# HGRN's heads taken two at a time, and a shorter triangle solve for the sample, in a hybrid RWKV-7 / HGRN2 layer

## The chip, the cores and the metric

The kernel runs on one core of one Trainium2 chip. The metric is the device time of one execution in microseconds, median of several runs. A core has a matmul engine (TensorE, PE in the profile; PEld is its loading of weights), VectorE (DVE), ScalarE (ACT), GpSimd (POOL), and SyncE (SP), from whose queue the data transfers are issued.

## The reference

One decoder layer in float32, for a prompt of 2,048 tokens (one sequence) and for a sample of 8 sequences of 8 new tokens that bring states with them. The input goes through a projection of width 1,024 to 3,840, then through two mixers side by side: RWKV-7 with 8 heads of 64, and HGRN2 with 4 heads of 128. Their outputs are joined, projected, added to the input and normalised, and an MLP of width 4,096 with a squared ReLU follows. HGRN2 is, in chunks:

```python
dec = jnp.exp(jnp.where(mask[:, :, None], diff, -jnp.inf))
att = jnp.einsum('bhtk,bhsk,bhtsk->bhts', qc, kc, dec)
o = jnp.einsum('bhts,bhsv->bhtv', att, ic) + jnp.einsum('bhtk,bhkv->bhtv', qc * jnp.exp(bc), S)
S = jnp.exp(blast[:, :, 0, :])[..., None] * S + jnp.einsum('bhsk,bhsv->bhkv', kc * jnp.exp(blast - bc), ic)
```

RWKV-7 updates a matrix state token by token, S = S diag(w) + (S a) b' + v k', and reads y = S r. In chunks of tokens this needs the inverse of a unit triangular matrix for each chunk and head.

## The kernel before, in words

**Stages.** The prompt is cut into 4 blocks of 512 tokens (`NBLK`, `BT`); block 0 carries the sample's 64 tokens too. `gemm` computes the input projection, block by block, in the order of `SEQ` (low rank rows, RWKV's r, k, v by pairs of heads, HGRN's input i, then f and q of heads 0 and 1, g of these, and so on), and then the output projection (`out_proj`) of the four blocks. Each product is three matmuls of high and low halves (`xh`, `xl`, `wh`, `wl`). Beside it run the streams `rwkv` with its helpers and `hgrn`. After all of that the MLP runs (`mlp_phase`).

**Order.** The order of instructions on each engine is fixed when the kernel is built. Every stream is a generator that issues some instructions and yields; `Sched.run` keeps a clock for each engine from prices in ns (`em.ops`) and lets the ready stream of the best priority go on. The RWKV chain comes first, then HGRN, and the projection is the filling. `Ring` hands out tiles: `RAW` has 12 tiles of 512 columns for x, r, k, f, q, g; `MB` has 3 PSUM banks; `HT` has the two HGRN work tiles (`ht` in the profile). Prices: `em.mm(..., price=35)` for a small HGRN matmul, `RETILE` 115 for a new tile shape.

**HGRN.** `hgrn` (L1577) goes through the heads of a block in turn, and after block 0 through the sample (`hg_sample`). `hg_head` (L1339) makes the forget gate `fg` and, in place of f, the key K, then Q. The attention inside 128 tokens is built in levels: a first batch of matmuls (`within`, L1332: for 4 chunks of 128 tokens, 4 products of 32 columns) gives the diagonal, and level `lv` gives the pairs of blocks of 2^lv tokens. After each level half of Q's columns and half of K's are multiplied by products of the gate (on VectorE, K also on GpSimd, `em.either`), and `fsm` gets the products of neighbours on GpSimd. Levels 0 to 4 use `within` and a masked copy (`copy_predicated`, L1366) into `attd`; levels 5 and 6 use matmuls of 32 and of 64 columns whose results ScalarE copies. So a head has eight batches of small matmuls: the first, five of levels 0 to 4, and one each of levels 5 and 6. Behind the levels come the transpose of K, the state's update, the output, its norm and its gate.

**The reserve.** When head `SPARE_AT` = 3 of block 0 is reached, `smp["rest"]` becomes 4: from then on whoever takes a RAW tile (the evacuations, `evac_job` L695, and the loads of x, `x_loads` L432) leaves four, until `hg_sample` has taken four.

**RWKV.** Nine quads follow each other through one `Stage`: two per block, and the sample as the third. For each, rows are made (`rwkv_rows`), scores computed (`rwkv_scores`), the triangles solved (`rwkv_solve`, L983), and then the chain over chunks runs (`chain`, for the sample `sample_chain`). The solve works on 32x32 triangles with 31 steps of two VectorE instructions (the products into `tmp`, tile `rhsb` in the profile, and their sum into the triangle, tile `xt`), transposes, and a join of the two halves of a 64-token chunk by 32x32 matmuls. The sample's 64 tokens of a head take the same way, though only blocks of 8 tokens belong together.

Of the kernel before, what the change touches and what calls it, by code (L numbers as in the profile page):

```python
# [42 lines left out]
TAIL = {"PE": 213, "DVE": 135, "ACT": 160, "POOL": 75, "SP": 0}  # L43
BUBBLE = 127
RETILE = 115
STEPS = 8
# [287 lines left out]
def mixer_phase(tc, em, a, o, dram, z, banks, sch, begin):  # L334
    nc = tc.nc
# [5 lines left out]
    def tl(shape, name, dt=F32):  # L341
        return rpool.tile(shape, dt, name=name)
# [38 lines left out]
    ET = Ring(sch, [tl([128, 512], f"et{i}") for i in range(ET_N)])  # L381
    HT = Ring(sch, [tl([128, 512], f"ht{i}") for i in range(2)])
    att = tl([128, 512], "att")
    attd = tl([128, 4, 32], "attd")
    em.memset(att, 0.0)
# [27 lines left out]
    for h in range(4):  # L413
        em.memset(Sh[h], 0.0)
    fsms = [tl([128, 512], f"fsm{i}") for i in range(1)]
    rsts = [tl([128, 8], f"rst{i}") for i in range(1)]
    GST = Ring(sch, [tl([128, 16], f"gst{i}") for i in range(2)])
# [565 lines left out]
    def rwkv_solve(sg, nb):  # L983
# [8 lines left out]
        tmp = rhs2[0][64:128]  # L992
        for s in range(31):
            nt, ncol = 31 - s, s + 1
            tv = tmp[:, 0:nt * ncol].rearrange("p (t c) -> p t c", t=nt)
            em.tt(tv, A3[:, s + 1:32, s:s + 1].to_broadcast([64, nt, ncol]),
                  X3[:, s, 0:ncol][:, None, :].to_broadcast([64, nt, ncol]), OP.mult)
            em.tt(X3[:, s + 1:32, 0:ncol], X3[:, s + 1:32, 0:ncol], tv, OP.add)
            if s % SOLVE_STEP == SOLVE_STEP - 1:
                yield "on"  # L1000
        uf = sg.uv.rearrange("p c l x -> p (c l x)")
        x11, w = uf[0:32, 0:1024], uf[32:64, 0:1024]
        tr32(x11.rearrange("t (b c) -> t c b", c=32), X3[0:32].rearrange("b t c -> b c t"))
        for hf in range(2):
            hs = slice(32 * hf, 32 * hf + 32)
            tr32(xt[hs, :, hs].rearrange("c b t -> c t b"), X3[hs])
        yield

# [16 lines left out]
        MB.put(ps)  # L1025
        em.memset(uf[0:64], 0.0)
        em.memset(X3, 0.0)
        em.memset(X3.rearrange("p t c -> p (t c)")[:, 0:1024:33], 1.0)
        yield

# [300 lines left out]

    def within(ps, K, Q):  # L1332

        for c in range(4):
            for x in range(0, 128, 32):
                s = slice(c * 128 + x, c * 128 + x + 32)
                em.mm(ps[x:x + 32, c * 32:c * 32 + 32], K[:, s], Q[:, s], price=35)

    def hg_head(h, b):  # L1339
        yield from sch.wait(("h", b, h))  # L1340
        yield from sch.wait(("i", b))
        fsm, rst = fsms[0], rsts[0]
        q, f = units[b, "q", h], units[b, "f", h]
        its = [units[b, "i", m] for m in range(4)]
        fg, Q = yield from HT.get_all(2)
        em.act(fg, f, AF.Identity, scale=col(P_OML + h), bias=col(P_LBV + h))
        em.act(f, f, AF.Identity, scale=col(P_NOML + h), bias=col(P_OML + h))
        K = f
        em.stt(Q, q, 0.5, fg, OP.mult, OP.mult)
        ps = yield from MB.get()  # L1350
        within(ps, K, q)
        yield
        a3 = att.rearrange("p (c t) -> p c t", c=4)
        em.stt(attd, ps[:, 0:128].rearrange("p (c t) -> p c t", c=4), 0.5,
               cst[:, C_IC:C_IC + 32][:, None, :].to_broadcast([128, 4, 32]), OP.mult, OP.mult)
        MB.put(ps)
        RAW.put(q)
        yield
        cur, off, n = fg, 0, 512
        for lv in range(7):  # L1360
            hh = 1 << lv
            ps = yield from MB.get()
            if lv < 5:
                within(ps, K, Q)
                yield
                nc.vector.copy_predicated(attd, hmask[:, M_LV + 32 * lv:M_LV + 32 * lv + 32][:, None, :].to_broadcast([128, 4, 32]),  # L1366
                                          ps[:, 0:128].rearrange("p (c t) -> p c t", c=4))
                em.ops.append((DVE, 220))
                if lv == 4:
                    for x in range(0, 128, 32):  # L1370
                        em.act(a3[x:x + 32, :, x:x + 32], attd[x:x + 32], AF.Copy)
            else:
                for c in range(4):
                    for x in range(0, 128, 2 * hh):
                        em.mm(ps[x:x + hh, c * hh:c * hh + hh], K[:, c * 128 + x:c * 128 + x + hh], Q[:, c * 128 + x + hh:c * 128 + x + 2 * hh])
                yield
                for x in range(0, 128, 2 * hh):
                    em.act(a3[x:x + hh, :, x + hh:x + 2 * hh], ps[x:x + hh, 0:4 * hh].rearrange("p (c t) -> p c t", c=4), AF.Copy)
            MB.put(ps)
            Q4 = Q.rearrange("p (b x h) -> p b x h", x=2, h=hh)  # L1380
            K4 = K.rearrange("p (b x h) -> p b x h", x=2, h=hh)
            nbk = 512 // (2 * hh)
            fe = cur[:, off:off + n:2][:, :, None].to_broadcast([128, nbk, hh])
            fo = cur[:, off + 1:off + n:2][:, :, None].to_broadcast([128, nbk, hh])
            em.tt(Q4[:, :, 1, :], Q4[:, :, 1, :], fe, OP.mult)
            em.either(K4[:, :, 0, :], K4[:, :, 0, :], fo, OP.mult, E_LATE)
            noff = 0 if lv == 0 else off + n
            em.tt(fsm[:, noff:noff + n // 2], cur[:, off:off + n:2], cur[:, off + 1:off + n:2], OP.mult, eng=POOL)
            cur, off, n = fsm, noff, n // 2
            yield  # L1390
        ft = fsm[:, off:off + 4]
        kt = fg
        ps = yield from MB.get()
# [5 lines left out]
        MB.put(ps)  # L1399
        RAW.put(K)  # L1400
        yield
        hs = slice(h * 128, h * 128 + 128)
        ps = yield from MB.get()
        for c in range(4):
            s = slice(c * 128, c * 128 + 128)
            em.mm(ps[:, s], kt[:, s], its[c][:, hs])
        sr = fsm
        po = yield from MB.get()
# [33 lines left out]
        MB.put(po)  # L1442
        HT.put(Q)
        yield
# [12 lines left out]
        RAW.put(g, delay=ST_TIME)  # L1457
        HT.put(kt)
        yield "go"

    def hg_sample():
# [4 lines left out]
        fsm, rst = fsms[0], rsts[0]  # L1466
        fg, Q = yield from HT.get_all(2)
        qm, s0, s1, im = yield from RAW.get_all(4)
# [92 lines left out]
        RAW.put(s0, s1, im)  # L1561
        HT.put(kt, Qs)
        RAW.put(qm, smp["qf"], smp["g"])
# [13 lines left out]
    def hgrn():  # L1577
        for b in range(NBLK):
            for h in range(4):
                if (b, h) == (0, SPARE_AT):  # L1580
                    smp["rest"] = 4
                yield from hg_head(h, b)
            if b == 0:
                yield from hg_sample()
        GB.put((yield from MB.get()))
# [440 lines left out]
def _build(arrays):  # L2026
    import concourse.bacc as bacc

    nc = bacc.Bacc("TRN2", target_bir_lowering=False, num_devices=1)
    a = {k: nc.dram_tensor("in_" + k, v.shape, mybir.dt.from_np(v.dtype), kind="ExternalInput").ap()  # L2030
# [26 lines left out]
```

## Time and profile before

| what | value |
|---|---|
| median of 3 runs | 3001.71 us (3001.17 to 3005.76) |
| profiled execution, its own time | 2999.65 us |
| span from the first to the last instruction | 2997.5 us |
| mean granted TensorE clock, of the upper level | 0.989 |
| instructions | 54442 |
| data transfers | q1, issued by SP; 329.64 MB |

The profile is of one execution. Its span is what the views cut up; the execution's own time holds about 2 us around it. A busy share counts an engine's instructions from start to end; matmuls overlap, so their lengths add up to more than the busy time.

### The profile page before, as it was taken

Reading aid. Unit: us, or ns where it says so; the run is one execution under the profiler, and the core shown is the slowest. Engines: PE = TensorE matmul, PEld = TensorE weight load, DVE = VectorE, ACT = ScalarE, POOL = GpSimd, SP = SyncE. Lnnn points to the kernel's source line nnn. Section 1 sums busy time; section 2 is a strip of 40 time slices with the busy share of each in tenths; the row PEclk is TensorE's granted clock in tenths of the full one; section 3 lists DMA queues with packets and bytes.
Section 4 is the critical chain, followed back from the end, with each engine's and each line's share of the span. In section 5 each row is a group of like instructions: output and inputs, shape, how many; then the busy total and the mean of one; then the engine's idle time right before and its main releaser. Section 6 shows DMA issues by size and latency. Waiting matters only on the chain.

```text
span 2997.5 us, 54442 instructions
## 1 busy us (share of the span) xinstructions
PE 2908.9 (97%) x22334; PEld 2531.1 (84%) x22334; DVE 1943.3 (65%) x3742; ACT 972.3 (32%) x2013; POOL 458.5 (15%) x496
## 2 busy tenths in 40 slices
PE   8998999999999999989999999999999999999998
PEld 8888877768777777889999999989999999888887
DVE  5767767777696868763755566557546655855556
ACT  4354323343444334422322222222222222322222
POOL 3333101110111111324600000011000000200002
PEclk9999999999999999989999999999999999999999
DMA  7535444443343334247622212112322211332221
GB/s 263 182 107 182 139 148 133 119 149 107 99 142 114 117 108 151 83 131 228 216 86 100 71 64 64 61 46 99 116 64 71 64 57 57 99 106 85 71 84 67
DMA packets 168778, 333.12 MB, mean 111 GB/s; under 512 B 29456, under 2 KB 47120, under 8 KB 168528
## 3 DMA queue, kind: packets, MB, share of 16 engines
q1 hardware_dynamic: 168528, 329.64, 33.9%
q8 instruction: 175, 2.87, 0.4%
q14 instruction: 75, 0.61, 0.1%
HBM read 268.56 MB, written 61.01 MB: 110 GB/s over the span
## 4 chain that ended last, share of the span: by engine, by line
PE 74%; DVE 9%; issue 1%; DMA 1%; ACT 1%; POOL 0%; SPq 0%; DVEq 0%; POOLq 0%; ACTq 0%
PE bank L93 72%; DVE rhsb L152 2%; DVE xt L152 1%; PE bank L104 1%; DVE xt L980 1%; DVE rs L156 1%; DVE et L156 0%; DVE xl L152 0%; DVE et L875 0%; DMA out_rw_s<-sc 0%; DVE sc L152 0%; DMA rs<-in_xT 0%; DVE Sq L152 0%; DVE rs L152 0%; DMA rs<-in_shg 0%
## 5 line engine op out<-in xcount | busy, mean ns | idle before, releaser
L152 DVE TENSOR_TENSOR acc<-bank,acc 128x512 f32<-128x512 f32 (+1 forms) x534 | 364.3, 688 | 217.6 <-PE bank L93 217.3
L93 PE MATMUL bank<-hh,upl 128*128 128x384 f32 (+1 forms) x1536 | 494.9, 322 | 0.0
L93 PE MATMUL bank<-hh,uph 128*128 128x384 f32 (+1 forms) x1536 | 494.8, 322 | 0.0
L93 PE MATMUL bank<-hl,uph 128*128 128x384 f32 (+1 forms) x1536 | 494.6, 322 | 0.0
L93 PE MATMUL bank<-xh,wh 128*128 128x512 f32 (+1 forms) x1040 | 411.6, 396 | 8.6 <-ACT wh L108 6.6
L93 PE MATMUL bank<-wdh,uh 128*128 128x512 f32 (+1 forms) x1068 | 417.5, 391 | 0.0
L93 PE MATMUL bank<-wdh,ul 128*128 128x512 f32 (+1 forms) x1068 | 416.5, 390 | 0.0
L93 PE MATMUL bank<-wdl,uh 128*128 128x512 f32 (+1 forms) x1068 | 416.4, 390 | 0.0
L93 PE MATMUL bank<-xl,wh 128*128 128x512 f32 (+1 forms) x1040 | 370.5, 357 | 4.8 <-DVE xl L152 4.8
L108 ACT ACTIVATE rl<-bank 128x384 f32<-128x384 f32 (+1 forms) x192 | 89.1, 464 | 867.0 <-PE bank L93 867.0
L93 PE MATMUL bank<-xh,wl 128*128 128x512 f32 (+1 forms) x1040 | 364.2, 357 | 1.4 <-POOL wl L152 1.3
L93 PEld LDWEIGHTS bank<-hh,uph 128*128 128x128 f32 x1536 | 288.2, 188 | 2.6
L93 PEld LDWEIGHTS bank<-hl,uph 128*128 128x128 f32 x1536 | 288.3, 188 | 1.9
L93 PEld LDWEIGHTS bank<-hh,upl 128*128 128x128 f32 x1536 | 288.3, 188 | 0.0
L152 DVE TENSOR_TENSOR u<-rl 128x384 f32<-128x384 f32 (+1 forms) x192 | 100.4, 523 | 266.4 <-ACT rl L108 266.2
L93 PE MATMUL bank<-wh,xh 128*128 128x256 f32 (+1 forms) x816 | 249.8, 306 | 5.8 <-DVE rs L156 3.9
L93 PEld LDWEIGHTS bank<-xh,wh 128*128 128x128 f32 x1040 | 198.3, 191 | 49.5 <-issue 11.2
L93 PEld LDWEIGHTS bank<-wdh,ul 128*128 128x128 f32 (+1 forms) x1068 | 197.2, 185 | 45.4
L93 PE MATMUL bank<-wl,xh 128*128 128x256 f32 (+1 forms) x816 | 234.8, 288 | 0.3 <-POOL wl L152 0.3
L93 PE MATMUL bank<-wh,xl 128*128 128x256 f32 (+1 forms) x816 | 234.5, 287 | 0.0
L93 PEld LDWEIGHTS bank<-wdl,uh 128*128 128x128 f32 (+1 forms) x1068 | 197.4, 185 | 43.1
L93 PEld LDWEIGHTS bank<-wdh,uh 128*128 128x128 f32 (+1 forms) x1068 | 197.3, 185 | 42.6
(230 smaller groups left out, 4783.9 us busy)
## 6 DMA issues: line engine op xcount, KB each, us to landing
raw<-in_wup SPq DMA_DIRECT2D x96, 512.0 KB, 3.5
raw<-in_wdown SPq DMA_DIRECT2D x96, 512.0 KB, 4.4
wh<-h_w SPq DMA_DIRECT2D x156, 256.0 KB, 2.7
wl<-l_w SPq DMA_DIRECT2D x156, 256.0 KB, 3.0
raww<-in_wout SPq DMA_DIRECT2D x64, 256.0 KB, 2.9
raww<-in_win SPq DMA_DIRECT2D x52, 256.0 KB, 3.5
h_w<-wh SPq DMA_DIRECT2D x52, 256.0 KB, 2.3
l_w<-wl SPq DMA_DIRECT2D x52, 256.0 KB, 2.2
```

What stands on the lines that cost most here:

```text
L93: self.nc.tensor.matmul(out, lhsT, rhs, start=start, stop=stop, skip_group_check=skip)
L104: self.nc.tensor.transpose(out, in_, ident)
L108: self.nc.scalar.activation(out, in_, func, **kw)
L152: (self.nc.vector if eng == DVE else self.nc.gpsimd).tensor_tensor(out, a, b, op=op)
L156: self.nc.vector.scalar_tensor_tensor(out, a, s, b, op0=op0, op1=op1)
L980: nc.vector.transpose(out, in_)
```

## The change

HGRN now goes through a block's heads by pairs (`hg_pair`): gate, K and Q of two heads lie in one sequence of 1,024 columns, in a triple of new `HT` tiles, K in its own tile and no longer in that of f. Each level has one batch of twice as many small matmuls, one masked copy and one update each of Q, K and `fsm`, of double width. What follows the levels is done head by head as before, from slices. The triple goes back when both heads are done. `SPARE_AT` now acts when the pair that holds head 3 begins. For the sample, the solve runs seven steps over four blocks of eight tokens at a time, in place of 31 steps, and the join is left out (its quarter of the tile is set to zero). The scratch for DMA descriptors is 1,024 bytes in place of the default. The planner's price of a small HGRN matmul goes from 35 to 14 ns.

```diff
-    HT = Ring(sch, [tl([128, 512], f"ht{i}") for i in range(2)])
-    att = tl([128, 512], "att")
-    attd = tl([128, 4, 32], "attd")
+    HT = Ring(sch, [[tl([128, 1024], f"ht{i}") for i in range(3)]])
+    att = tl([128, 1024], "att")
+    attd = tl([128, 8, 32], "attd")
...
-    fsms = [tl([128, 512], f"fsm{i}") for i in range(1)]
+    fsms = [tl([128, 1024], f"fsm{i}") for i in range(1)]
...
-        for s in range(31):
+
+        def blocks(ap, t, c, *dims):
+
+            ap = ap.rearrange("p a b -> p (a b)")
+            return bass.AP(tensor=ap.tensor, offset=ap[:, t * 32 + c:t * 32 + c + 1].offset, ap=[ap.ap[0], [8 * 32 + 8, 4], *dims])
+
+        for s in range(7 if nb == 8 else 0):
+
+            nt, ncol = 7 - s, s + 1
+            tv = tmp[:, 0:4 * nt * ncol].rearrange("p (b t c) -> p b t c", b=4, t=nt)
+            em.tt(tv, blocks(A3, s + 1, s, [32, nt], [0, ncol]), blocks(X3, s, 0, [0, nt], [1, ncol]), OP.mult)
+            x = blocks(X3, s + 1, 0, [32, nt], [1, ncol])
+            em.tt(x, x, tv, OP.add)
+            yield "on"
+        for s in range(0 if nb == 8 else 31):
...
+        if nb > 8:
+            tr32(x11.rearrange("t (b c) -> t c b", c=32), X3[0:32].rearrange("b t c -> b c t"))
...
+            yield from rwkv_join(xt, sb, x11, w, nb)
+        else:
+            em.memset(xt[0:32, 0:nb, 32:64], 0.0)
...
-    def within(ps, K, Q):
-
-        for c in range(4):
+    def hg_pair(h0, b):
+
+        hds = (h0, h0 + 1)
+        for h in hds:
+            yield from sch.wait(("h", b, h))
+        yield from sch.wait(("i", b))
+        fsm = fsms[0]
+        its = [units[b, "i", m] for m in range(4)]
+        fg, Q, K = ht = yield from HT.get()
+        for i, h in enumerate(hds):
+            f = units[b, "f", h]
+            s = slice(512 * i, 512 * i + 512)
+            em.act(fg[:, s], f, AF.Identity, scale=col(P_OML + h), bias=col(P_LBV + h))
+            em.act(K[:, s], f, AF.Identity, scale=col(P_NOML + h), bias=col(P_OML + h))
+            RAW.put(f)
+        for i, h in enumerate(hds):
+            s = slice(512 * i, 512 * i + 512)
+            em.stt(Q[:, s], units[b, "q", h], 0.5, fg[:, s], OP.mult, OP.mult)
+        ps = yield from MB.get()
+        qs = [units[b, "q", h] for h in hds]
+        for c in range(8):
             for x in range(0, 128, 32):
-                s = slice(c * 128 + x, c * 128 + x + 32)
-                em.mm(ps[x:x + 32, c * 32:c * 32 + 32], K[:, s], Q[:, s], price=35)
-
-    def hg_head(h, b):
-        yield from sch.wait(("h", b, h))
-        yield from sch.wait(("i", b))
-        fsm, rst = fsms[0], rsts[0]
-        q, f = units[b, "q", h], units[b, "f", h]
-        its = [units[b, "i", m] for m in range(4)]
-        fg, Q = yield from HT.get_all(2)
-        em.act(fg, f, AF.Identity, scale=col(P_OML + h), bias=col(P_LBV + h))
-        em.act(f, f, AF.Identity, scale=col(P_NOML + h), bias=col(P_OML + h))
-        K = f
-        em.stt(Q, q, 0.5, fg, OP.mult, OP.mult)
-        ps = yield from MB.get()
-        within(ps, K, q)
-        yield
-        a3 = att.rearrange("p (c t) -> p c t", c=4)
-        em.stt(attd, ps[:, 0:128].rearrange("p (c t) -> p c t", c=4), 0.5,
-               cst[:, C_IC:C_IC + 32][:, None, :].to_broadcast([128, 4, 32]), OP.mult, OP.mult)
+                e = (c % 4) * 128 + x
+                em.mm(ps[x:x + 32, c * 32:c * 32 + 32], K[:, c * 128 + x:c * 128 + x + 32], qs[c // 4][:, e:e + 32], price=WITHIN)
+        yield
+        a3 = att.rearrange("p (c t) -> p c t", c=8)
+        em.stt(attd, ps[:, 0:256].rearrange("p (c t) -> p c t", c=8), 0.5,
+               cst[:, C_IC:C_IC + 32][:, None, :].to_broadcast([128, 8, 32]), OP.mult, OP.mult)
         MB.put(ps)
-        RAW.put(q)
-        yield
-        cur, off, n = fg, 0, 512
+        RAW.put(*qs)
+        yield
+        cur, off, n = fg, 0, 1024
         for lv in range(7):
             hh = 1 << lv
             ps = yield from MB.get()
             if lv < 5:
-                within(ps, K, Q)
+                for c in range(8):
+                    for x in range(0, 128, 32):
+                        s = slice(c * 128 + x, c * 128 + x + 32)
+                        em.mm(ps[x:x + 32, c * 32:c * 32 + 32], K[:, s], Q[:, s], price=WITHIN)
                 yield
-                nc.vector.copy_predicated(attd, hmask[:, M_LV + 32 * lv:M_LV + 32 * lv + 32][:, None, :].to_broadcast([128, 4, 32]),
-                                          ps[:, 0:128].rearrange("p (c t) -> p c t", c=4))
-                em.ops.append((DVE, 220))
+                nc.vector.copy_predicated(attd, hmask[:, M_LV + 32 * lv:M_LV + 32 * lv + 32][:, None, :].to_broadcast([128, 8, 32]),
+                                          ps[:, 0:256].rearrange("p (c t) -> p c t", c=8))
+                em.ops.append((DVE, 350))
                 if lv == 4:
                     for x in range(0, 128, 32):
                         em.act(a3[x:x + 32, :, x:x + 32], attd[x:x + 32], AF.Copy)
             else:
-                for c in range(4):
+                for c in range(8):
                     for x in range(0, 128, 2 * hh):
-                        em.mm(ps[x:x + hh, c * hh:c * hh + hh], K[:, c * 128 + x:c * 128 + x + hh], Q[:, c * 128 + x + hh:c * 128 + x + 2 * hh])
+                        em.mm(ps[x:x + hh, c * hh:c * hh + hh], K[:, c * 128 + x:c * 128 + x + hh], Q[:, c * 128 + x + hh:c * 128 + x + 2 * hh],
+                              price=WITHIN if lv == 5 else 106)
                 yield
                 for x in range(0, 128, 2 * hh):
-                    em.act(a3[x:x + hh, :, x + hh:x + 2 * hh], ps[x:x + hh, 0:4 * hh].rearrange("p (c t) -> p c t", c=4), AF.Copy)
+                    em.act(a3[x:x + hh, :, x + hh:x + 2 * hh], ps[x:x + hh, 0:8 * hh].rearrange("p (c t) -> p c t", c=8), AF.Copy)
             MB.put(ps)
             Q4 = Q.rearrange("p (b x h) -> p b x h", x=2, h=hh)
             K4 = K.rearrange("p (b x h) -> p b x h", x=2, h=hh)
-            nbk = 512 // (2 * hh)
+            nbk = 1024 // (2 * hh)
             fe = cur[:, off:off + n:2][:, :, None].to_broadcast([128, nbk, hh])
             fo = cur[:, off + 1:off + n:2][:, :, None].to_broadcast([128, nbk, hh])
             em.tt(Q4[:, :, 1, :], Q4[:, :, 1, :], fe, OP.mult)
@@ -1388,8 +1420,14 @@
             em.tt(fsm[:, noff:noff + n // 2], cur[:, off:off + n:2], cur[:, off + 1:off + n:2], OP.mult, eng=POOL)
             cur, off, n = fsm, noff, n // 2
             yield
-        ft = fsm[:, off:off + 4]
-        kt = fg
+        for i, h in enumerate(hds):
+            s = slice(512 * i, 512 * i + 512)
+            yield from hg_head(h, b, its, K[:, s], Q[:, s], fg[:, s], att[:, s], fsm[:, off + 4 * i:off + 4 * i + 4],
+                               fsm[:, 384 * i:384 * i + 384], rsts[0][:, 8 * i:8 * i + 8])
+        HT.put(ht)
+        yield "go"
+
+    def hg_head(h, b, its, K, Q, kt, att, ft, sr, rst):
...
-                if (b, h) == (0, SPARE_AT):
+            for h in range(0, 4, 2):
+                if b == 0 and SPARE_AT in (h, h + 1):
                     smp["rest"] = 4
-                yield from hg_head(h, b)
+                yield from hg_pair(h, b)
...
-    nc = bacc.Bacc("TRN2", target_bir_lowering=False, num_devices=1)
+    nc = bacc.Bacc("TRN2", target_bir_lowering=False, num_devices=1, dynamic_dma_scratch_size=1024)
```

## Rows read from the trace of the kernel before

**Rows 1.** The profile's page, busy time, share of the span and instructions of each engine

```profile
PE 2908.9 (97%) x22334; PEld 2531.1 (84%) x22334; DVE 1943.3 (65%) x3742; ACT 972.3 (32%) x2013; POOL 458.5 (15%) x496
```

**Rows 2.** Stages, us: length, busy (x) PE, PEld, DVE, ACT, POOL; clock, DMA share, GB/s

```profile
100.00:1255.00 1155.00, 1100.70 (x11689) 880.67 (x11685) 858.00 (x2087) 467.85 (x1167) 215.86 (x293) 0.99 0.41 130
1255.00:1335.00 80.00, 69.42 (x663) 65.56 (x664) 61.62 (x115) 21.60 (x54) 26.44 (x23) 0.85 0.41 127
1335.00:1495.00 160.00, 156.95 (x1366) 152.44 (x1365) 83.85 (x128) 50.99 (x96) 87.68 (x66) 0.99 0.64 210
1495.00:2997.00 1502.00, 1494.10 (x7957) 1349.75 (x7955) 887.91 (x1274) 381.67 (x600) 93.22 (x72) 1.00 0.24 77
```

**Rows 3.** TensorE's waits from 100 to 1340 us: total us, times, longest

```profile
PE bank L93 <- DVE et L156: 7.2, 6, 1.8
PE bank L93 <- DVE ht L152: 6.9, 6, 1.7
PE bank L93 <- DVE rs L156: 5.9, 2, 3.9
```

**Rows 4.** TensorE's timeline, 126.5 to 128.5 us: start, length, instruction, count

```profile
126.89 0.29 PE L93 MATMUL bank<-xl,wh 128*128 128x288 f32 x1
127.02 0.29 PE L93 MATMUL bank<-xh,wl 128*128 128x288 f32 x1
127.24 0.46 PE L93 MATMUL bank<-rs,rs 128*32 128x32 f32 x32
...
127.87 0.30 PE L93 MATMUL bank<-xl,wh 128*128 128x288 f32 x1
```

**Rows 5.** TensorE's timeline, 781.5 to 785 us

```profile
781.64 0.40 PE L93 MATMUL bank<-uv,sc 128*64 128x64 f32 x8
...
782.70 0.39 PE L93 MATMUL bank<-xl,wh 128*128 128x512 f32 x1
...
783.93 0.45 PE L93 MATMUL bank<-uv,sc 128*64 128x64 f32 x8
...
784.65 0.39 PE L93 MATMUL bank<-xl,wh 128*128 128x512 f32 x1
```

**Rows 6.** The HGRN tiles' matmuls: count, ns min/median/max, first and last start

```profile
L93 PE MATMUL bank<-ht,rs x2968: 189/196/270, 131.3 to 1257.0; 128*32 128x32 f32 x188, 128*64 128x64 f32 x10
```

**Rows 7.** VectorE by line and shape, 100 to 1300 us: busy us, mean ns

```profile
L152 DVE TENSOR_TENSOR ht<-ht,fsm 128x256 f32<-128x256 f32 x96 | 42.3, 441 | 8.5 <-PE bank L93 4.7 <-POOL wl L152 3.0 <-issue 0.4
...
L152 DVE TENSOR_TENSOR rs<-rs,fsm 128x512 f32<-128x512 f32 x8 | 5.5, 686 | 0.4 <-PE bank L93 0.4
```

**Rows 8.** VectorE's timeline, 507.0 to 508.4 and 779.8 to 781 us

```profile
507.16 0.70 DVE L156 SCALAR_TENSOR_TENSOR bk<-bk,et 128x512 f32<-128x512 f32 x1
507.78 0.68 DVE L152 TENSOR_TENSOR bk<-bk,et 128x512 f32<-128x512 f32 x1
...
779.90 0.30 DVE L1366 COPY_PREDICATED attd<-hmask,bank 128x128 f32<-128x128 uint8 x1 [0.62 <-PE bank L93]
780.11 0.42 DVE L152 TENSOR_TENSOR ht<-ht,fsm 128x256 f32<-128x256 f32 x1
780.44 0.42 DVE L152 TENSOR_TENSOR rs<-rs,fsm 128x256 f32<-128x256 f32 x1
```

**Rows 9.** The triangle tile in the sample's solve, 425 to 505 us

```profile
L152 DVE TENSOR_TENSOR rhsb<-xt x31: 189/371/698, 429.3 to 493.9; 64x31 f32<-64x31 f32 x2, 64x60 f32<-64x60 f32 x2, 64x87 f32<-64x87 f32 x2, 64x112 f32<-64x112 f32 x2
...
L93 PE MATMUL bank<-xt,uv x16: 236/236/258, 503.4 to 503.6; 32*32 32x32 f32 x16
...
L980 DVE STREAM_TRANSPOSE uv<-xt x1: 2107/2107/2107, 494.3 to 494.3; 32x1024 f32<-32x1024 f32 x1
```

**Rows 10.** The sample's stretch, busy us as in rows 2

```profile
425.00:508.00 83.00, 77.75 (x566) 54.44 (x565) 71.85 (x157) 28.09 (x58) 14.18 (x20) 0.98 0.49 157
```

**Rows 11.** SP's queue, loads of block 1's x, 265 to 312 us

```profile
298.11 4.65 SPq L173 DMA_DIRECT2D rs<-in_xT  x3
...
307.65 0.38 SPq L173 DMA_DIRECT2D rs<-in_xT  x1
```

## What the change will do to the time

> **What bounds the kernel now.** I read four things in order. First the busy shares: TensorE is busy for 97% of the span, VectorE for 65% [rows 1]. Then the span cut into stages; the granted clock is near its upper level in all but one of them [rows 2]. From 1495 us on the MLP leaves TensorE 8 us idle in 1502: nothing of this change is there, and nothing can be won. From 100 to 1255 us, where RWKV, HGRN and the input projection share the engines, TensorE is idle for 1155 - 1100.7 = 54.3 us. From 1255 to 1335 us, where the last triangle solve runs beside the output projection, it is idle for 10.6 us and the clock is at 0.85 of its upper level of 2.4 GHz. From 1335 to 1495 us it is idle for 3 us. Third, who lets TensorE wait before 1340 us [rows 3]: VectorE in nearly every large entry, 7.2 us for `et`, 6.9 us for `ht` (the HGRN tiles), 5.9 us for `rs`. So TensorE's own list of work sets the time. A VectorE saving counts only where TensorE stands waiting for VectorE, and a shorter RWKV chain only as far as it closes a gap.
>
> The fourth view, TensorE's timeline, shows that being busy is not all streaming. Two neighbouring projection matmuls start 0.13 us apart (126.89, 127.02). When one batch of HGRN's 32-column matmuls (16 matmuls, recorded as 32) is put between two of them, 0.85 us pass from the last projection matmul before (127.02) to the second one after (127.87) [rows 4]. Without the batch that would be 0.27 us, so the batch costs 0.58 us. Its records overlap: the batch lasts 0.46 us and one record 0.196 us (median), so records follow each other every (0.46 - 0.196) / 31 = 8.5 ns, and 32 of them stream for 0.27 us [rows 4, 6]. The other 0.31 us is paid for going into another tile shape and out of it.
>
> **The change part by part.**
>
> *Half as many batches.* Each head issues eight batches: the first, five levels at 32 columns, one level with 32-wide blocks and one with 64-wide ones. 16 heads make 128, pairs make 64 of double size. The number of matmuls stays. A pair's batch between projection matmuls costs 0.58 + 0.27 = 0.85 us against 2 x 0.58 = 1.16: 0.31 saved. Where the batch stands beside other small tiles it shares a switch that happens anyway: from the `uv,sc` batch at 781.64 through the HGRN batch to the second projection matmul (782.70) are 1.06 us, and from `uv,sc` at 783.93 with no HGRN batch to the same point (784.65) 0.72 us [rows 5]. The batch adds 0.34 us there, two add 0.68, a pair's 0.61: 0.07 saved. Bounds are 64 x 0.07 = 4.5 us and 64 x 0.31 = 20 us. I take 0.22 each, nearer the upper, since projection matmuls are the bulk of TensorE's list around the batches: **-14 us**. The planner's price of a batch, 16 x 35 ns before and 32 x 14 for the double one, moves no work; it only shifts the order, which I cost at nothing and leave to the rivals.
>
> *VectorE work per level.* By mean durations two 256-column updates (0.441 each) against one of 512 (0.686) save 0.20 us [rows 7]. The starts say less: updates start 0.33 us apart at 256 columns (780.11, 780.44) and 0.62 at 512 (507.16, 507.78), so merging two saves 0.04 us; the masked copy occupies 0.21 us (779.90 to 780.11) and would occupy 0.21 + 0.29 / 2 = 0.355 at double width (0.29 us being what 256 further columns cost an update), which saves 0.065 [rows 8]. Seven levels with two updates and five copies in eight pairs make 56 x 2 x 0.04 + 40 x 0.065 = 7 us of VectorE by the starts, and over 22 by the durations. I take the starts, since a queue of instructions is delayed by spacing. The Trainium skill's page Perfetto Trace Analysis, section Optimizing Scalar/DVE Operations, gives about 60 ns of overhead per VectorE instruction on SBUF and says that the profiled latency is about twice this. By it 112 removed updates would give 7 us; the starts agree with that within a factor of two.
>
> *The sample's solve.* It is 62 instructions of 0.37 us (median), spread from 429.3 to 494 us, then a transpose of 2.1 us that goes too, and a join that begins at 503.4 us [rows 9]. Seven steps of two instructions, with at most 64 elements, cost about 0.19 us each, the shortest of those rows: 2.7 us for 23, and 2.1 more for the transpose, so 22 us of VectorE less. The sample's chain can start some 55 us sooner. The join's two TensorE batches go: at most 2 x 0.58, I take **-1 us**. The memset that is added runs on GpSimd, which is 15% busy [rows 1].
>
> *What VectorE's relief is worth.* In all it loses 29 us of the 858 between 100 and 1255 [rows 2]. HGRN's own waits (6.9 us, six times) come half as often, each perhaps longer: 0 to -7, I take **-4**. In the sample's stretch from 425 to 508 us TensorE is idle for 83 - 77.75 = 5.25 us and the clock is at 0.98, worth 1.7 us [rows 10]: 0 to -7, I take **-3**. Other waits for VectorE [rows 3], from `et` and `rs` to the smaller ones, shrink by a few per cent up to a third: 0 to -5, **-2**.
>
> *The RWKV chain moved forward.* After 1335 us TensorE is dense whether the chain ends sooner or not, so the 55 us themselves are worth nothing. What can go are the gaps of 1255 to 1335 us: 10.6 us idle and 0.15 x 80 = 12 us by the clock [rows 2], if the last solve moves under input projection. That is 0 to -22; the planner may spend the lead earlier, and I take **-6**.
>
> *Tiles.* K no longer lies in the RAW tile of `f`, which is free right after two ScalarE instructions. Against that, four RAW tiles are reserved for the sample from the moment the pair (2, 3) of block 0 is begun, a whole head earlier than now. Behind that reserve stand block 1's x loads, which are issued up to 307 us now [rows 11], and the evacuations of block 0's last heads on ScalarE; the projection waits for both. The cost is 0 if the freed tiles make up for it, and up to 15 us (the loads from the first at 298 wait till the pair has used its inputs, and the clock falls); I take **+4**. The smaller DMA scratch costs nothing here: every data transfer is issued from SP's queue, and GpSimd's is not used. ScalarE is 32% busy and issues fewer block copies; its row stays covered by TensorE [rows 1].
>
> Sum: -14 - 1 - 4 - 3 - 2 - 6 + 4 = **-26 us**. The profiled execution took 2999.65 us (its span 2997.5 and 2 us around it), so 2974 us; the median of the runs shown lies 2 us above it. I forecast **2975 us**. Adding all the good ends gives -62 us, all the bad ones +10.
>
> **Rivals.**
>
> *Waits take the saving back, slower than before.* A level of a pair holds TensorE's next batch for two 512-column updates and a wider copy: 2 x 0.29 + 0.145 = 0.725 us longer per level than a head's [rows 8]. TensorE's order is fixed by the planner, whose prices for these come from the same formulas as before. Were no projection matmul left to put in between, 56 levels x 0.725 = 41 us would be added, against 26 saved: **3015 us**. It decides from about 36 uncovered levels on. Against it: of the 112 levels of the 16 heads only six now show a wait on `ht`, in all 6.9 us [rows 3]. The Trainium skill (Perfetto Trace Analysis, Optimizing Scalar/DVE Operations) states the general form: where VectorE is not saturated but makes bubbles on others, breaking instructions up may let work finish sooner. VectorE at 65% with TensorE waiting for it is that case, and the rule would undo this change.
>
> *The reserve stalls block 1.* The same sum with +15 for +4, and no gain at the end of the mixer: 2999.65 - 14 - 1 - 4 - 3 - 2 + 15, about 2991; with the switches at their low bound 3000, which is **no change**.
>
> *The end gap closes whole.* The lead of 55 us carries through to the last solve and -22 stands in place of -6, with the switches at -20: -48, **2953 us**.
>
> *The change does little on TensorE*, because most batches stand beside small tiles: -4.5 for -14, all else as summed: **2985 us**.
>
> **How the numbers follow.** Chances: forecast, with its own range of 2962 to 2988 that takes in the fourth rival, 0.62; end gap closes 0.14; reserve stalls 0.15; waits take it back 0.09. A difference below 0.2%, some 6 us, is about what a measurement of this kernel can't tell from none. Of the stall case I give 0.10 to no change and 0.05 to faster. Faster 0.62 + 0.14 + 0.05 = 0.81; same 0.10; slower 0.09. The range of 2949 to 2999 leaves out the slower case and the outermost of the good ends.
>
> **What would show it.** In the new profile: 64 records in a 32-column batch, of about 0.7 us, and half as many batches; between projection matmuls 0.85 us of cost. The masked copy at about 0.44 us with half the count; the sample's solve done within 15 us of its start; TensorE's busy time before 1500 us about 15 us smaller and its idle time 8 to 15 smaller. In 1255 to 1335 us and its counterpart the clock nearer to 1. The forecast is wrong if TensorE's waits for `ht` grow beyond 15 us, if a gap of over 5 us opens where block 1's x is loaded, or if a pair's batch takes as long as two.

## The result, and the profile after

The change makes the kernel slower: 3026.97 us (median of 4 runs, 3020.11 to 3028.92) against 3001.44 us, ratio 1.008, 95% interval 1.006 to 1.01. The forecast was 2975 us.

What was foreseen on TensorE is there. One batch of 64 records stands between two projection matmuls (TensorE's timeline of the changed kernel: start, length, instruction):

```profile
141.06 0.29 PE L95 MATMUL bank<-xh,wl 128*128 128x288 f32 x1
141.29 0.76 PE L95 MATMUL bank<-rs,ht 128*32 128x32 f32 x64
141.98 0.40 PE L95 MATMUL bank<-xh,wh 128*128 128x288 f32 x1
142.22 0.29 PE L95 MATMUL bank<-xl,wh 128*128 128x288 f32 x1
```

From 141.06 to the second projection matmul after the batch (142.22) are 1.16 us; without the batch 0.27. It costs 0.89 us (0.85 was forecast), where two single batches cost 2 x 0.58 [rows 4]. The busy shares answer to [rows 1], and the sample's solve to [rows 9]: seven steps in 16 us of wall time in place of 31 in 65.

```profile
PE 2903.5 (96%) x22302; PEld 2538.1 (84%) x22302; DVE 1929.4 (64%) x3559; ACT 954.3 (32%) x1935; POOL 435.5 (14%) x429
```

```profile
L154 DVE TENSOR_TENSOR rhsb<-xt x7: 185/206/924, 448.2 to 464.5; 64x28 f32<-64x28 f32 x2, 64x48 f32<-64x48 f32 x2, 64x60 f32<-64x60 f32 x2, 64x64 f32<-64x64 f32 x1
```

TensorE is busy 5 us less over the whole span, and the span is 21 us longer (3018.3 against 2997.5 us). Stages of the changed kernel, as in [rows 2] (busy times of PE, PEld, DVE, ACT, POOL; clock; DMA share; GB/s):

```profile
640.00:675.00 35.00, 32.83 (x406) 28.43 (x406) 17.03 (x36) 11.10 (x45) 5.32 (x7) 0.95 0.31 107
675.00:711.00 36.00, 25.22 (x225) 20.97 (x224) 15.07 (x42) 10.33 (x31) 1.84 (x2) 0.58 0.05 16
...
1335.00:1513.00 178.00, 166.63 (x1592) 159.12 (x1592) 94.32 (x147) 53.33 (x108) 86.32 (x68) 0.97 0.57 189
1513.00:3018.00 1505.00, 1496.89 (x7966) 1352.58 (x7964) 889.31 (x1277) 383.81 (x603) 94.73 (x72) 1.00 0.23 77
```

The MLP takes what it took; it begins 19 us later (1513.4 against 1494.3 us). Up to there TensorE is idle for 106.4 us against 80.2, at a mean clock of 0.96 against 0.98. The place to look is 675 to 711 us: a clock of 0.58, near the lower level, hardly any DMA, and VectorE and ScalarE idle for more than half of it. What TensorE did there, and whom it waited for (groups of that stretch: busy us, mean ns; idle before, and until whom):

```profile
L95 PE MATMUL bank<-uv,sc 128*64 128x64 f32 x72 | 5.5, 300 | 0.0
L95 PE MATMUL bank<-ar,bk 64*128 64x128 f32 x32 | 4.5, 437 | 1.4 <-DVE pc L167 1.0 <-DVE sc L154 0.4
L95 PE MATMUL bank<-Sq,ar 128*128 128x128 f32 x16 | 4.3, 414 | 4.2 <-DVE Sq L154 4.2
...
L95 PE MATMUL bank<-uv,bkt 128*64 128x64 f32 x40 | 3.2, 309 | 3.4 <-DVE uv L167 3.4
```

That is RWKV's chain of one quad alone, step after step, with nothing to put into its waits. Apart from a handful at 675 the input projection is missing for 36.0 us. ScalarE's and TensorE's timelines at its end tell why (`itk<-bank` evacuates the `i` projection that was computed up to 675):

```profile
705.50 0.69 ACT L110 ACTIVATE vx<-bank,pp 128x512 f32<-128x512 f32 x1
706.08 1.20 ACT L110 ACTIVATE itk<-bank 128x256 f32<-128x256 f32 x4
```

```profile
707.47 2.07 PE L95 MATMUL bank<-ar,bk 64*128 64x128 f32 x14 [0.43 <-DVE sc L154]
709.47 1.95 PE L106 MATMUL bank<-cst,bk 128*128 128x128 f32 x8
711.23 0.62 PE L106 MATMUL bank<-cst,vx 128*128 128x128 f32 x4
711.61 0.36 PE L95 MATMUL bank<-wh,xh 128*128 128x256 f32 x1
```

Evacuations go in order. The one of `v` (`vx<-bank`) needs one of three VX tiles, and gets it when the next quad is scored; behind it stands `itk`, and behind that the banks that the projection needs. In the kernel before the same `v` was evacuated at 706.50 us, but the projection arrived there only at 705.55 us (ScalarE's and TensorE's timelines of the kernel before):

```profile
706.50 0.70 ACT L108 ACTIVATE vx<-bank,pp 128x512 f32<-128x512 f32 x1
```

```profile
705.55 0.28 PE L93 MATMUL bank<-wh,xl 128*128 128x256 f32 x1
```

Now it arrives 30 us early and stops.

TensorE's waits from 0 to 1514 us ([rows 3] begins at 100): `ht` took 8.9 us in 4 waits against 6.9 in 6 in the kernel before, `et` 20.4 in 13 against 11.4 in 8. A wait for the first rows of the MLP's input (`acc`) is new in this size; it was 2.6 us.

```profile
PE bank L95 <- DVE et L158: 20.4, 13, 3.7
PE bank L106 <- DVE acc L158: 10.3, 2, 7.7
PE bank L95 <- DVE rs L158: 9.6, 3, 3.7
PE bank L95 <- DVE ht L154: 8.9, 4, 4.6
```

### The profile page after: what moved, and what is told of

Same layout as the page of the kernel before. It is cut to its first block, busy times and chain, and to the rows that moved or that the text cites. A ratio compares the mean times of both kernels' runs of the same rounds, so it can differ in the third digit from the quotient of the medians.

```text
span 3018.3 us, 53967 instructions
## 1 busy us (share of the span) xinstructions
PE 2903.5 (96%) x22302; PEld 2538.1 (84%) x22302; DVE 1929.4 (64%) x3559; ACT 954.3 (32%) x1935; POOL 435.5 (14%) x429
## 4 chain that ended last, share of the span: by engine, by line
PE 52%; DMA 1%; DVE 1%; issue 0%; POOL 0%; SPq 0%; ACT 0%; POOLq 0%; DVEq 0%; ACTq 0%
PE bank L95 51%; DMA raww<-in_wout 1%; PE bank L106 1%; DVE acc L158 0%; POOL wl L154 0%; SPq L175 0%; DMA acc<-z 0%; DMA rs<-oT 0%; DVE st L1797 0%; DVE hl L154 0%; DVE rs L158 0%; DVE upl L154 0%; DVE xl L154 0%; DVE acc L154 0%; ACT hh L110 0%
```

## The experiments

All are timed beside runs of the kernel before; differences are between medians of runs made together (the kernel before: 2998 to 3001 us), with the ratio's 95% interval. "Holes" are stretches of over 4 us from the end of one projection matmul to the start of the next, up to the MLP, added up from the trace: 52.7 us in the kernel before, 89.4 in the changed one. A quad (b, q) is one of the two halves of RWKV's heads in block b.

**Which part?** First each part alone.

```diff
# e1: the pairs alone
-        for s in range(7 if nb == 8 else 0):
+        for s in range(7 if nb == 0 else 0):
...
-        for s in range(0 if nb == 8 else 31):
+        for s in range(31):
...
-        if nb > 8:
+        if nb:
# e2: the kernel before with rwkv_solve and rwkv_join of the changed one
```

Expected of e1: 

> The pair of heads alone; the sample is solved and joined as before. Theory A (the pairs do it: their denser VectorE work stretches the RWKV solve beside them and the projection, relieved on TensorE, reaches the ring of three v tiles before the chain has freed one): 3018 to 3032 us, and TensorE without projection work for 20 us or more somewhere between 600 and 760 us. Theory B (the sample's short solve does it, by pulling the first RWKV quads and all that is planned behind them out of step): 2980 to 2995 us, no such hole. By the terms of the prediction, which add up: about 2982 us.

Expected of e2: 

> The sample's eight-token solve alone, with HGRN by single heads as before. Theory A: 2990 to 3002 us, since without the pairs nothing stretches the quad behind the sample. Theory B: 3012 to 3030 us, with the hole at 640 to 720 us. By the prediction's terms (the sample's stretch -3, the chain forward -6, a join's matmuls -1): about 2991 us.

Measured: e1 3042.72 us, +43.3 (1.0132 to 1.0162); e2 2994.79 us, -4.6 (0.9976 to 0.9996). The pairs, at price 14, lose, as theory A said, but more than its 3018 to 3032 us and more than the whole change does: holes of 147 us, one of 51.9 us from 531 on, beside the sample's chain, one of 36.2 from 700 on.

**The ring, or the price?**

```diff
# e3: changed kernel
-    VX = Ring(sch, [tl([128, 512], f"vx{i}") for i in range(3)])
+    VX = Ring(sch, [tl([128, 512], f"vx{i}") for i in range(4)])
# e5: kernel before
-                em.mm(ps[x:x + 32, c * 32:c * 32 + 32], K[:, s], Q[:, s], price=35)
+                em.mm(ps[x:x + 32, c * 32:c * 32 + 32], K[:, s], Q[:, s], price=14)
```

Expected of e3: 

> The changed kernel with four v tiles in the ring in place of three. If the ring is what stops the projection at 675 us (theory A): the hole of 36 us shrinks to under 15 us and the time falls by 12 to 25 us, to 3002 to 3015 us. If the RWKV chain is the bound whatever the ring holds (theory C): the hole comes back later, by as much, and the time stays at 3020 to 3032 us.

Expected of e5: 

> The kernel before, with the planner's price of a 32-column matmul set from 35 to the 14 that the change uses; nothing else, so the same instructions in another planned order. Theory D (the new price reorders the work and the loss is the order's): 3012 to 3030 us. Theories A and B: 2995 to 3007 us.

Measured: e3 3024.09 us, +24.7 (1.0066 to 1.0096), the same as with three tiles. The hole has gone from 675 and come back at 1394 us, 48.3 us long, where the output projection waits for the last chain:

```profile
1394.00:1443.00 49.00, 22.02 (x177) 15.62 (x177) 18.78 (x43) 7.40 (x22) 5.13 (x6) 0.57 0.16 54
```

So theory A falls in its second half: the ring is only where the projection happens to stop, and the run came out as theory C said. e5 is 3014.68 us, +15.3 (1.004 to 1.007): the price alone, on the same matmuls, costs more than half of what the change does, as theory D said.

**The old price, shorter VectorE instructions, HGRN's priority.**

```diff
# f1
-WITHIN = 14
+WITHIN = 35
# f2: per head (the mask copy and K's product likewise)
-            em.tt(Q4[:, :, 1, :], Q4[:, :, 1, :], fe, OP.mult)
+            for i in range(2):
+                s = slice(512 * i, 512 * i + 512)
+                Q4 = Q[:, s].rearrange("p (b x h) -> p b x h", x=2, h=hh)
...
# f3: HG_PRIO
-EV_PRIO, HG_PRIO, PREP_PRIO, ROWS_PRIO, POST_PRIO = 0, 1, 3, 1, 1
+EV_PRIO, HG_PRIO, PREP_PRIO, ROWS_PRIO, POST_PRIO = 0, 3, 3, 1, 1
```

Expected of f1: 

> The changed kernel with the planner's price of a 32-column matmul back at 35. If the new price makes the order that loses (it cost the kernel before 15 us): 3003 to 3015 us. If the pairs lose by themselves: 3022 to 3035 us.

Expected of f2: 

> The changed kernel with each level's VectorE updates (mask copy, Q and K product) issued per head again, 512 columns an instruction, while the 32-column matmuls stay batched by pairs. If the long instructions stand in the way of RWKV's short steps on VectorE: 3000 to 3012 us. If it is the bunching of two heads, whatever the length of an instruction: 3022 to 3040 us.

Expected of f3: 

> The changed kernel with HGRN planned at priority 3, behind RWKV's scores and solve, instead of 1. If the pairs hold RWKV's solve up by standing ahead of it on VectorE: the solve of 567 to 639 us falls under 60 us and the time goes to 3000 to 3015 us. If not: 3020 to 3035 us.

Measured: f1 2983.69 us, **-16.1** (0.993 to 0.9959), better than either explanation allowed. With the price at 35 the change gains, inside the range that was forecast. `WITHIN` also prices level 5, which the kernel before prices by its columns, at 106 ns, and the mask copy and level 6 have new prices as well; so f1 does not bring back the old planning in all, and e5 changes only the six batches that cost 35 before. f2 3024.39 us, +24.6 (1.0071 to 1.0105): the length of the instructions is not it. (An update of Q or K touches half of its columns: 512 for a pair, and in f2 256 for a head, not the 512 of its expectation.) f3 2996.15 us, -3.7 (0.9982 to 1.0002), 29 us less than the changed kernel's +25.5: at price 14 the lower priority helps much. But not as was expected: the solve still takes 61 us (568.0 to 629.4), and the hole is even longer (45.6 us from 655 on) and at a low clock:

```profile
655.00:701.00 46.00, 34.72 (x327) 29.17 (x328) 22.18 (x62) 15.96 (x52) 3.05 (x4) 0.67 0.07 24
```

The same stretch as in the changed kernel at price 35 (f1) is dense and at full clock:

```profile
640.00:711.00 71.00, 70.11 (x680) 59.66 (x678) 43.67 (x112) 27.21 (x83) 6.95 (x9) 1.00 0.32 101
```

One thing that the price moved is seen on VectorE in the solve of quad (1, 0), which took 72 us from 567.0 on (after every two steps, that is four instructions, the planner may put in something else). Timeline of the changed kernel:

```profile
595.59 0.42 DVE L154 TENSOR_TENSOR rhsb<-xt 64x255 f32<-64x255 f32 x1
...
596.96 0.42 DVE L154 TENSOR_TENSOR xt<-xt,rhsb 64x256 f32<-64x256 f32 x1
597.41 0.69 DVE L154 TENSOR_TENSOR xl<-rs,xh 128x512 fp32r<-128x512 f32 x1
598.02 0.68 DVE L154 TENSOR_TENSOR et<-bank,vx 128x512 f32<-128x512 f32 x1
598.62 0.43 DVE L1397 COPY_PREDICATED attd<-hmask,bank 128x256 f32<-128x256 uint8 x1
598.95 1.29 DVE L154 TENSOR_TENSOR ht<-ht,fsm 128x512 f32<-128x512 f32 x2
600.27 0.42 DVE L154 TENSOR_TENSOR rhsb<-xt 64x255 f32<-64x255 f32 x1
```

Between one pair of steps (its last instruction starts at 596.96) and the next (600.27) stand two instructions of the projection and of RWKV and a whole level of an HGRN pair. Groups of that solve's window, first of the changed kernel (567 to 639 us), then of f1 (562 to 619 us):

```profile
L154 DVE TENSOR_TENSOR ht<-ht,fsm 128x512 f32<-128x512 f32 x11 | 7.5, 723 | 1.6 <-PE bank L95 1.6
L1397 DVE COPY_PREDICATED attd<-hmask,bank 128x256 f32<-128x256 uint8 x5 | 2.2, 440 | 0.9 <-PE bank L95 0.9
```

```profile
L154 DVE TENSOR_TENSOR ht<-ht,fsm 128x512 f32<-128x512 f32 x6 | 3.9, 683 | 0.0
...
L1397 DVE COPY_PREDICATED attd<-hmask,bank 128x256 f32<-128x256 uint8 x4 | 1.8, 445 | 0.1
```

At 14 there are eleven updates and waits for TensorE inside the solve, at 35 there are six and next to no wait, and the solve takes 56 us. This solve alone does not make the loss: f3 keeps ten of the updates in its solve, and loses nothing.

**How the price acts.**

```diff
# h1: the edit of e1, and
-WITHIN = 14
+WITHIN = 35
# h2 (h3: 24)
-WITHIN = 14
+WITHIN = 50
# h4: in hg_pair, all three places
-price=WITHIN
+price=35 if b == 1 else WITHIN
# j1: the edit of e5, with price=50
```

Expected of h1: 

> The pair of heads alone, the sample solved and joined as before, at the planner's old price of 35. If the parts add up (both parts 2983.7 us, the sample's part alone -4.6): 2984 to 2993 us. If the pairs pay only where the sample's solve is short: 2998 us or more.

Expected of h2: 

> The changed kernel with a price of 50. If a higher price works as a brake, by letting fewer projection matmuls in ahead of RWKV's steps: the holes without projection stay near 66 us or shrink, and the time is 2970 to 2988 us. If each price only gives another order by luck: anywhere from 2975 to 3030 us, with holes to match.

Expected of h3: 

> The changed kernel with a price of 24. If the price is a brake: between the 2983.7 us at 35 and the 3027 us at 14, so 2990 to 3020 us, with holes between 66 and 89 us. If it is luck: outside of that is as likely as inside.

Expected of h4: 

> The changed kernel with 35 for the HGRN pairs of block 1 alone, 14 elsewhere. If the loss is made where the hole is seen, in the planning of block 1's pairs beside the solve of 567 to 639 us: 2983 to 2998 us, the hole of 36 us gone. If it is made over the whole mixer or in block 0: 3012 to 3030 us.

Expected of j1: 

> The kernel before with a price of 50 for its 32-column matmuls. If 35 already holds its projection and RWKV in step: 2995 to 3010 us, and the 16 us at price 35 belong to the change. If it too gains from a stronger brake: 2982 to 2994 us, and a price alone gives much of what the change gives.

| price | changed kernel | holes, us | kernel before |
|---|---|---|---|
| 14 | +25.5 us (1.006 to 1.01) | 89.4 | +15.3 us (e5) |
| 24 | +4.5 us (1.0002 to 1.002, h3) | 95.7 | |
| 35 | -16.1 us (f1) | 66.0 | 0 |
| 50 | -12.8 us (0.9933 to 0.9968, h2) | 60.6 | +5.3 us (1.0009 to 1.0031, j1) |

The time falls with the price up to 35 and then stays, as a brake would have it; four points don't rule out luck. The holes follow badly: h3 has more of them than the changed kernel, outside of the 66 to 89 expected, with a solve of 71 us and a hole of 37.9 us from 670 on, and yet loses only 4.5 us; e5 has 126.6 us of them and loses 15.3. The 16 us at 35 belong to the change, as far as the kernel before shows at its three prices: it gains nothing at 50. h4 is 3017.88 us, +17.5 (1.0033 to 1.0064): the price in block 1 alone shortens the hole to 20.7 us and gives back 8 of 42 us, so the loss is made over the mixer, not in that one place. The starts of the solves say the same: in the changed kernel those of blocks 1 to 3 begin 5, 19, 26, 27, 42 and 37 us later than in f1 (567.0, 722.9, 863.6, 1000.6, 1139.1 and 1288.9 us against 562.0, 704.2, 838.1, 973.9, 1097.3 and 1252.4). h1 is 3013.36 us, +13.0 (1.0022 to 1.0049), against the 2984 to 2993 of adding up: the pairs lose even at 35 where the sample's solve is long. The two parts together gain 24 us more than their sum (-16.1 against 13.0 - 4.6).

**Does RWKV set the end?** Here every second step of the prompt quads' solves is left out, so RWKV gets shorter and no work is taken from TensorE (the computation is incomplete in these three). The solve now yields after each of its 16 steps, where it yielded after every second of 31, so other work can come between about as often as before.

```diff
# g1: kernel before
-        for s in range(31):
+        for s in range(0, 31, 2) if nb > 8 else range(31):
# i1: changed kernel; i2: changed kernel, WITHIN = 35
-        for s in range(0 if nb == 8 else 31):
+        for s in [] if nb == 8 else range(0, 31, 2):
# all three
-            if s % SOLVE_STEP == SOLVE_STEP - 1:
+            if s % SOLVE_STEP == SOLVE_STEP - 1 or nb > 8:
```

Expected of g1: 

> The kernel before, with every second of the 31 steps of the solve left out for the eight quads of the prompt (so part of the computation is missing): each solve of 37 to 65 us loses some 20 us, and nothing is taken from TensorE. If TensorE's own list sets the time, as the prediction says, a shorter RWKV chain gives back only the gaps at 1255 to 1335 us: 6 to 22 us, to 2979 to 2995 us. If the succession of RWKV quads (scores, solve, chain, one Stage) is what sets the mixer's end: 30 to 55 us, to 2945 to 2970 us.

Expected of i1: 

> The changed kernel (price 14) with every second step of the prompt quads' solve left out, as in the run on the kernel before (part of the computation is missing). If the price loses because the projection outruns RWKV: the hole of 36 us closes, the time falls by 50 us or more, to 2955 to 2975 us, and lies within 10 us of the next run. If the order of price 14 loses on TensorE whatever RWKV takes: 2985 to 3005 us, 25 us or more above the next run.

Expected of i2: 

> The same with the price at 35 (part of the computation is missing here too). Both explanations: 2955 to 2968 us, the 27 us that the kernel before lost by this edit taken off 2983.7 us, less what its smaller holes can't give.

Measured: g1 2972.82 us, -27.0 (0.9899 to 0.9929), between the two expectations; i2 2959.89 us, -40.8 (0.9847 to 0.9876); i1 2950.29 us, **-50.4** (0.9813 to 0.9846). With short solves the low price is not the worse one but the better by 10 us, and the hole at 675 is gone. So the order that price 14 makes does not lose on TensorE whatever stands beside it; it loses beside solves of full length. The halved solves also take 87 us of work off VectorE before the MLP (busy 1054.7 us in the kernel before and 967.8 in g1, 1040.5 in the changed kernel and 954.0 in i1). Whether it is RWKV's succession of steps that can't keep up, or VectorE's load, no run tells apart.

The rows behind it: RWKV's chain steps (`Sq,ar`, the last start is the last quad's last step) and the MLP's first matmul (first start). Kernel before:

```profile
L93 PE MATMUL bank<-Sq,ar x32: 273/275/421, 1316.8 to 1357.8; 128*128 128x128 f32 x32
...
L93 PE MATMUL bank<-hh,uph x1536: 288/334/343, 1494.3 to 2960.5; 128*128 128x384 f32 x128, 128*128 128x288 f32 x64
```

The changed kernel, then f1, then g1, then i1:

```profile
L95 PE MATMUL bank<-Sq,ar x44: 270/275/377, 1240.0 to 1381.9; 128*128 128x128 f32 x44
...
L95 PE MATMUL bank<-hh,uph x1536: 288/334/667, 1513.4 to 2981.2; 128*128 128x384 f32 x128, 128*128 128x288 f32 x64
```

```profile
L95 PE MATMUL bank<-Sq,ar x32: 270/275/348, 1306.7 to 1344.6; 128*128 128x128 f32 x32
...
L95 PE MATMUL bank<-hh,uph x1536: 288/334/668, 1476.4 to 2943.4; 128*128 128x384 f32 x128, 128*128 128x288 f32 x64
```

```profile
L93 PE MATMUL bank<-Sq,ar x32: 270/275/377, 1259.6 to 1298.7; 128*128 128x128 f32 x32
...
L93 PE MATMUL bank<-hh,uph x1536: 288/334/343, 1466.9 to 2933.1; 128*128 128x384 f32 x128, 128*128 128x288 f32 x64
```

```profile
L95 PE MATMUL bank<-Sq,ar x32: 270/275/348, 1263.4 to 1305.9; 128*128 128x128 f32 x32
...
L95 PE MATMUL bank<-hh,uph x1536: 288/334/343, 1446.0 to 2912.5; 128*128 128x384 f32 x128, 128*128 128x288 f32 x64
```

From the last step to the MLP are 131.5 us in the changed kernel, 131.8 in f1, and 131.5 in h1 (1371.0 and 1502.5). It is 136.5 in the kernel before, and 168.2 in g1, 140.1 in i1, 164.9 in i2 (1293.8 and 1458.7). This tail is not a wait: TensorE idles 11 of its 131.5 us in the changed kernel. It is the output projection that the planned order leaves behind the last step: 894 records of it in the changed kernel and in f1, 930 in h1, 1014 in the kernel before, 1272 in g1. In e3, where TensorE did wait for the last chain, only the last block's 384 are left, and the tail is 105.3 us. So the equal tails do not show by themselves that RWKV's end sets the time. What shows how far the end follows is g1: there RWKV ends 59 us sooner and the MLP begins 27 us sooner, and the longer list behind the last step takes up the rest.

**What is left at price 35.**

```diff
# all: WITHIN = 35; i3: HG_PRIO 3 as in f3; i4: four VX tiles as in e3; k1:
-APART = 4000.0
+APART = 2000.0
```

Expected of i3: 

> The changed kernel with price 35 and HGRN at priority 3. If the priority, as the price does, only keeps the projection and RWKV in step: little is left to gain, 2978 to 2990 us. If it clears VectorE for RWKV's solve besides: 2965 to 2978 us. If the two brakes overshoot: over 2990 us.

Expected of i4: 

> The changed kernel with price 35 and four v tiles. If the ring bounds it once the price is right: 2968 to 2979 us. If a larger ring only lets the projection run further ahead of RWKV (as with four tiles at price 14, whose hole came at 1394 us): 2984 to 3010 us, with a hole near the mixer's end.

Expected of k1: 

> The changed kernel with price 35, and the loads that prepare the MLP planned 2 us apart (APART) instead of 4, so that the first blocks of its input come sooner. If the wait of 8.5 us at the MLP's entry is a load issued too late: it closes, and the time is 2973 to 2979 us. If it hangs on the output projection's rows, or the earlier loads hold up others on SP's queue: 2981 to 2988 us.

Measured: i3 2989.03 us, -11.7 (0.9953 to 0.9979), little left for the priority, though the solve of quad (1, 0) now takes only 38 us; i4 2995.3 us, -5.4 (0.9973 to 0.9991), a larger ring makes it 11 us worse, without the late hole that was expected. k1 2975.66 us, **-22.9** (0.9912 to 0.9939): faster than both kernels, and 7 us of it is the wait at the MLP's entry. TensorE's waits from 1340 us to the MLP, in f1 and then in k1, where no wait for `acc` is left:

```profile
PE bank L106 <- DVE acc L158: 11.2, 2, 8.5
PE bank L95 <- POOL wl L154: 0.7, 1, 0.7
```

```profile
PE bank L95 <- POOL wl L154: 2.5, 2, 2.1
```

## Why the prediction was wrong

**The step that failed** is one sentence: "The planner's price of a batch, 16 x 35 ns before and 32 x 14 for the double one, moves no work; it only shifts the order, which I cost at nothing and leave to the rivals." The order is worth 42 us (+25.5 for the changed kernel, -16.1 for f1), more than all the terms together, and no rival was about it. In place of 0 stands +42; without it the change measures -16 where the sum said -26, inside the forecast's range. The sentence also leaves out that level 5's price fell from 106 to 14. The three signs that the prediction named for being wrong do not show (`ht` waits of 8.9 us, no gap of over 5 us where block 1's x is loaded, 0.89 us for a pair's batch against 1.16 for two): they were about the terms, not about the order.

**Behind it stands a second one:** "TensorE's own list of work sets the time", and "the 55 us themselves are worth nothing". By the halved solves the kernel before was close to a balance of two bounds: the projection's list on TensorE, and the succession of RWKV quads through one Stage (scores, solve, chain), with VectorE's part in it. The 97% of [rows 1] don't show the second, since the projection fills its waits. g1 shows what ending RWKV 59 us sooner is worth: 27 us, a little over the 22 that the prediction allowed at most. The rest is argued, not shown: what TensorE saves makes the projection run ahead of RWKV, and what is planned ahead of the solve on VectorE makes RWKV later; both turn into holes at a low clock, and then into a later end of the last chain. Against a simple form of it stand f3 and h3, which have such holes and lose little or nothing.

**Term by term.** Switches, -14: 39 of 64 batches stand between matmuls of full 128x128 tiles (74 of 128 before, counted in the traces), which gives 74 x 0.58 - 39 x 0.89 = 8 us, and by the prediction's 0.34 and 0.61 for the others 54 x 0.34 - 25 x 0.61 = 3: an estimate of -11. VectorE: updates of 512 columns follow each other after 0.60 us and those of 256 after 0.34 (medians), so each merge saves 0.07 us, not the 0.04 read from [rows 8], whose 0.62 begins with an instruction of RWKV. HGRN's own waits, -4: +2. Other waits for VectorE, -2: from 100 to 1340 us those for `et` alone rose from 7.2 to 16.1. The sample's part, -1, -3 and -6: -4.6 measured alone (e2). The reserve, +4: block 1's loads of x were issued by 288 us, sooner than in [rows 11]; nothing. The wait at the MLP's entry was not foreseen: 8 us, and k1 takes it away.

**The rivals.** The slower one came out on the right side by luck, for another reason: it wanted `ht` waits of 41 us, and there are 8.9, and pairs with updates of a single head's length (f2) are no faster. The Trainium skill's rule that it named (Perfetto Trace Analysis, Optimizing Scalar/DVE Operations, breaking instructions up) gives nothing here: +24.6 us split, +25.5 not.

**Open.** That a lower price puts HGRN's levels between the steps of the solve is seen in one solve, and f3 gains without taking them out; how the planner comes from the price to each order was not followed. What share of the 42 us is level 5's price was not run. Why the pairs need the short solve of the sample at price 35 is argued from the same balance, not shown.

## What to carry to other kernels

A constant that only an order is planned by is part of the change: cost it, and time the change with the old value too. When a busy engine is fed by a filler (here the projection) around a serial chain, look for what sets the chain's end before pricing a saving on the engine: cut the chain short in a trial run, and see how far the end follows. A saving on one of two balanced bounds pays in full only if the other moves along. A trial run that cuts the chain should take nothing else with it; here it also relieved VectorE.

## What was not expected of the hardware

TensorE fell to near the lower of its two clock levels while it was busy for 25.22 of 36 us with small matmuls of the chain, between waits: the granted clock of 675 to 711 us is 0.58, and the chain's `Sq,ar` records take 414 ns on the mean against a median of 275 over the whole run. At 640 to 711 us in f1 the same chain steps stand among projection matmuls and the clock is 1.00.
